# Reordering one recurrence step of a hybrid encoder kernel: a constant's load, the group norm's loads and buffers, and one piece of fill

## The chip, the cores and the metric

The kernel runs on one core of a Trainium2 chip. The metric is the device time of one execution in microseconds (us). The verdict between two kernels is the median of repeated runs. The profile is a hardware trace of one further execution.

The engines are TensorE (PE, matrix products), VectorE (DVE), ScalarE (ACT), GpSimd (POOL) and SyncE (SP). SP computes nothing here: it issues nearly all DMA transfers, one after the other, and when one of them has to wait, all behind it wait too.

## The reference, cut to what matters

One layer of an encoder is computed for 1024 + 256 = 1280 tokens of width 1024: a token mixer (a gated convolution and a bidirectional RWKV-7 recurrence, 8 heads of size 64), a gated feed-forward net and a gated embedding. The part around the change is the recurrence and the group norm of its result:

```python
def step(S, inp):
    r_t, w_t, kk_t, b_t, k_t, v_t = inp
    sa = jnp.einsum('bhvk,bhk->bhv', S, kk_t)
    S = (S * w_t[:, :, None, :] - sa[..., None] * b_t[:, :, None, :]
         + v_t[..., None] * k_t[:, :, None, :])
    return S, jnp.einsum('bhvk,bhk->bhv', S, r_t)
...
y = outs[0] + outs[1]
mean = jnp.mean(y, axis=-1, keepdims=True)
var = jnp.mean(jnp.square(y - mean), axis=-1, keepdims=True)
y = ((y - mean) * lax.rsqrt(var + GN_EPS)).reshape(bsz, T, D_RWKV) * gn_w + gn_b
bonus = jnp.sum(heads(r32) * heads(k32) * r_k, axis=-1, keepdims=True) * heads(v32)
g = jax.nn.sigmoid(gd.astype(f32)) @ gate_g2
out = (y + bonus.reshape(bsz, T, D_RWKV)) * g
```

## The kernel before, in words

The recurrence runs in chunks of 64 tokens. A step of the kernel handles two chunks (128 tokens) of one direction; there are 20 steps `n`: ten forward (0 to 9), then ten backward (10 to 19). They take the stretch from 337.5 us (the first product of step 0) to about 905 us of the trace.

Within a chunk the sequential sum is turned into products with the inverse of a triangular matrix. This inverse is made two steps ahead, in a chain that crosses four engines:

- `a_gram(n+2)`: PE makes Gram products (`g<-LS,K`), DVE masks them into `AT`, `LS` and `ZL`. SP stores `AT` to a scratch array `dA` (4 DMAs).
- `load_u(n+2)`: SP loads `dA` back as `U` in another layout (4 DMAs), and loads `W`, a constant that holds unit rows, from `in_consts`.
- `b_inv(n+2)`: POOL works in place on `W`, 31 pairs of a product (`tm<-W,U`) and a sum (`W<-W,tm`).
- `b_out(n+1)`, `b_back(n+1)`, in step `n`: SP stores `W` to `dW` (4 DMAs) and loads it as `MT` (4 DMAs).
- `b_d(n+1)`, later in step `n`: DVE transposes two blocks of `MT` into `Dm`.
- `b_x2(n+1)`: the first thing PE does in step `n+1`, `g<-Dm,AT`, reads `Dm`.

The step itself handles its two chunks with `c_p1`, `c_sa` and `c_z` (`ci` is 0, then 1). `c_p1` multiplies the state `SV` with `LS`, and ACT copies the result to `R`. `c_sa` multiplies `R` with `MT`, and ACT copies that into `SV` (`SV<-p`). `c_z` multiplies `SV` with `ZL`, and DVE makes the next state (`Sc<-p,Sc`, `SV<-Sc,pend`).

Between these pieces stands "fill": other projections of the layer (`mm<-U,wh`, `mm<-U,wl`), which depend on nothing in the recurrence. `gap(us, 1)` puts `us` worth of fill into PE's program, in pieces of about 0.8, and after each piece runs one more part of a Python generator `gn`. The total of the fill over a step is fixed by `share`; 18.6 is the sum of the arguments of a step's gaps.

From step 11 on, the generator is `group_norm`: each step normalizes the 128 tokens that the backward direction finished in the step before. It works on four 128x512 tiles: `y` and `y2` (the halves of the buffer tagged `cvp`), `v` and `q` (the halves of `cvy`). `gn_load` allocates both buffers and loads all four at the end of a step. The result goes into `y2` and from there to `d_ob`. Since the buffers are allocated anew, with one buffer for each tag, a load into them waits until the tile before is released.

The order of every engine is the order in which the Python code emits it (the wrapper `Pin` keeps program order). All instructions go through one helper, so the trace shows line L204 for all; they are told apart by their tiles.

Of the kernel before, what the change touches and what calls it, by code (L numbers as in the profile page):

```python
# [5 lines left out]
F32 = mybir.dt.float32  # L6
F32R = mybir.dt.float32r
AF = mybir.ActivationFunctionType
ALU = mybir.AluOpType
# [7 lines left out]
DC = 512  # L17
# [16 lines left out]
C_WI = C_BO + 128  # L34
C_N = C_WI + 256
# [24 lines left out]
class B:  # L60
# [5 lines left out]
    def sb(self, pool, shape, dt=F32, tag=None, bufs=None):  # L66
        kw = {} if bufs is None else dict(bufs=bufs)
        return pool.tile(shape, dt, name=tag, tag=tag, **kw)
# [57 lines left out]
def build(tc, I, O, dbg=None, upto=99):  # L126
    b = B(tc, I, O)
    nc = tc.nc
    sb = b.sb
    V, A, G, PE, SP = nc.vector, nc.scalar, nc.gpsimd, nc.tensor, nc.sync  # L130
# [45 lines left out]
    d_v, d_g = dram([2, T, 256], "d_v"), dram([2, T, 256], "d_g")  # L176
    d_y = [dram([2, T, 256], f"d_y{d}") for d in range(2)]
    d_ob = dram([T, DC], "d_ob")
# [13 lines left out]
    bon = sb(cp, [128, NT, 8], F32, "bon")  # L192
# [867 lines left out]
    st = {}  # L1060
# [39 lines left out]
    def a_gram(n, h):  # L1100
        d, g = steps[n]
        S = st[n]
        if h == 0:
            if n < 3:
                ZL[n] = sb(wk, [128, 2, 8, 128], F32, f"ZL{n}")
            S["AT"] = sb(wk, [128, 8, 64], F32, "AT", 3)
            S["dA"] = dr.tile([32, 32, 32], F32, name="dA", tag="dA", bufs=2)
        K, L, Zl, AT = S["K"], LS[n % 4], ZL[n % 3], S["AT"]
        bc = lambda c: cst[:, c:c + 64].unsqueeze(1).broadcast_to((128, 4, 64))
        MS, MQ = bc(C_MS[d]), bc(C_MQ[d])  # L1110
        pss = [sb(pg, [128, 4, 128], F32, "g") for par in range(2)]
        us = slice(4 * h, 4 * h + 4)
        for u in range(4):
            for par in range(2):
                rw = halves[par]
                PE.matmul(pss[par][:, u, :], K[rw, 4 * h + u, :], L[rw, par::2 - par, 4 * h + u, :], start=True, stop=True)
        cc, qc = slice(0, 64), slice(64, 128)
        for par in range(2):
            rw, ow, co, qo, ps = halves[par], halves[1 - par], par * 64, (1 - par) * 64, pss[par]
            V.tensor_tensor(AT[rw, us], ps[rw, :, cc], MS[rw], ALU.mult)  # L1120
            V.tensor_tensor(L[ow, par, us], ps[ow, :, cc], MS[ow], ALU.mult)
            V.tensor_tensor(Zl[:, par, us, qo:qo + 64], ps[:, :, qc], MQ, ALU.mult)
            if h == 1:
                for hh in range(2):
                    q = par * 2 + hh
                    SP.dma_start(S["dA"][q * 8:q * 8 + 8].rearrange("u s t -> s u t"), AT[q * 32:q * 32 + 32, :, hh * 32:hh * 32 + 32])
# [10 lines left out]
    def load_u(n):  # L1137
        Ut = st[n]["U"] = sb(wk, [128, 32, 32], F32, "U", 2)
        for r in range(4):
            SP.dma_start(Ut[r * 32:(r + 1) * 32], st[n]["dA"])  # L1140
        st[n]["W"] = sb(wk, [128, 8, 32], F32, "W", 2)
        SP.dma_start(st[n]["W"], I["consts"][:, C_WI:C_N].rearrange("p (c j) -> p c j", c=8))


    def b_inv(n):
# [137 lines left out]
            SP.dma_start(t[:, par * 256:(par + 1) * 256].rearrange("p (h v) -> p h v", v=64),  # L1283
                         I[nm][0].rearrange("(h p v) -> p h v", p=2, v=64)[par].unsqueeze(0).broadcast_to((128, 4, 64)))

    def gn_load(g):
        tk = slice(g * 128, (g + 1) * 128)
        ya, yb = sb(wq, [128, 2, DC], F32, "cvp"), sb(wq, [128, 2, DC], F32, "cvy")
        t4 = ya[:, 0], ya[:, 1], yb[:, 0], yb[:, 1]
        for t, src in zip(t4, (d_y[0], d_y[1], d_v, d_g)):  # L1290
            SP.dma_start(t.rearrange("t (q m) -> t q m", q=2), src[:, tk, :].rearrange("q t m -> t q m"))
        return t4

    def group_norm(g, t4):
        tk = slice(g * 128, (g + 1) * 128)
        y, y2, v, q = t4
        h8 = lambda t: t.rearrange("p (h v) -> p h v", v=64)
        bc = lambda t: t.unsqueeze(2).broadcast_to((128, 8, 64))
        V.tensor_tensor(y, y, y2, ALU.add)
        yield  # L1300
        mean = sb(wg, [128, 8], F32, "gm", 2)
        V.tensor_reduce(mean, h8(y), mybir.AxisListType.X, ALU.add)
        V.tensor_scalar(mean, mean, 1.0 / 64, None, ALU.mult)
        yield
        V.tensor_tensor(h8(y), h8(y), bc(mean), ALU.subtract)
        yield
        A.activation(y2, y, AF.Square)
        yield
        yield
        var = sb(wg, [128, 8], F32, "gv", 2)  # L1310
        V.tensor_reduce(var, h8(y2), mybir.AxisListType.X, ALU.add)
        V.tensor_scalar(var, var, 1.0 / 64, 64e-5, ALU.mult, ALU.add)
        V.tensor_tensor(h8(v), h8(v), bc(bon[:, g, :]), ALU.mult)
        yield
        s = sb(wg, [128, 8], F32, "grs")
        A.activation(s, var, AF.Sqrt)
        yield
        rs = b.newton(wg, var, s, 8, "gr", V)
        yield
        V.tensor_tensor(h8(y), h8(y), bc(rs), ALU.mult)  # L1320
        yield
        V.tensor_tensor(y, y, gnw, ALU.mult)
        yield
        V.tensor_tensor(y, y, gnb, ALU.add)
        yield
        V.tensor_tensor(y, y, v, ALU.add)
        yield
        pq = lambda t: t.rearrange("t (p h v) -> t p h v", p=2, v=64)
        V.tensor_tensor(y2.rearrange("t (h p v) -> t p h v", p=2, v=64), pq(y), pq(q), ALU.mult)
        SP.dma_start(d_ob[tk, :], y2)  # L1330

    go(9.0)
    for h in range(2):
# [25 lines left out]
    def gap(us, g=0):  # L1359
        k = max(1, round(us / 0.8))  # L1360
        for _ in range(k):
            fill.run(us * share / k)
            if g:
                next(gn, None)

    for n in range(N):
        share = max(0.0, fill.left - TAIL) / (N - n) / 18.6
        nx, nx2 = n + 1 < N, n + 2 < N
        run_side()
        load_l(n + 3)  # L1370
        b_x2(n)
        c_p1(n, 0)
        gap(1.3)
        if n >= 11:
            gn = group_norm(gl_g, gl_t)
        b_m21(n)
        c_keep(n, 0)
        if nx2:
            a_gram(n + 2, 0)
        gap(0.6)  # L1380
        c_sa(n, 0)
        if nx2:
            a_gram(n + 2, 1)
        gap(1.0)
        c_z(n, 0)
        if nx2:
            load_u(n + 2)
            b_inv(n + 2)
        gap(1.6, 1)
        c_p1(n, 1)  # L1390
        c_keep(n, 1)
        if nx2:
            a_t(n + 2)
        load_k(n + 3)
        if nx:
            b_out(n + 1)
        gap(1.0, 1)
        c_sa(n, 1)
        if nx:
            b_back(n + 1)  # L1400
        gap(1.5, 1)
        c_z(n, 1)
        fill.until(v_block + 1)
        if nx2:
            load_v(n + 2)
        gap(4.9, 1)
        if nx:
            b_d(n + 1)
        gap(6.7, 1)
        for _ in gn:  # L1410
            pass
        if n >= 10:
            gl_g = steps[n][1]
            gl_t = gn_load(gl_g)
    close(wk, pa, pg)


# [640 lines left out]
```

## Time and profile before

| | us |
|---|---|
| runs, without profile | 2200.03, 2207.47, 2580.53 |
| median of these | 2207.47 |
| the profiled execution | 2213.88 |
| its span, from the first to the last instruction | 2212.1 |

| engine | busy us | share of the span |
|---|---|---|
| PE | 2140.0 | 97% |
| DVE | 1343.1 | 61% |
| ACT | 888.4 | 40% |
| POOL | 520.5 | 24% |

The mean granted clock of TensorE is 0.989 of its full 2.4 GHz. Its lower level is 1.2 GHz, shown as 0.50. A row of the timeline gives the start and the length in us, the engine, the operation, out<-in by names, the shape and how many such instructions were merged; in brackets stands how long the engine was idle just before, and who ended that. A row of SPq is the issue of a DMA: its landing comes later. Where SP's row begins late, SP has waited.

### The profile page before, as it was taken

The page shows a single profiled execution, that of the slowest core. Times are in us where ns is not written, and L with a number is a line of the kernel's source. Part 1 is how long each engine was busy: PE and PEld are TensorE (multiplying, and loading weights), DVE is VectorE, ACT ScalarE, POOL GpSimd, SP SyncE. Part 2 cuts the span into 40 slices and gives each one's busy share as a digit, 9 for nine tenths or more (in the row PEclk, how much of TensorE's full clock was granted, in tenths as well). Part 3 has the DMA queues.
Part 4 walks back from the last instruction along what each step waited for, and adds up shares of the span by engine and source line. Part 5 has one row for each costly group of instructions (what it writes and reads, how often), then busy time and mean ns, then how long its engine had stood idle before and what let it go on. Part 6 is the DMA issues. An engine that isn't in the chain of part 4 may idle for free.

```text
span 2212.1 us, 40064 instructions
## 1 busy us (share of the span) xinstructions
PE 2140.0 (97%) x15929; PEld 1844.1 (83%) x15929; DVE 1343.1 (61%) x2198; ACT 888.4 (40%) x1529; POOL 520.5 (24%) x1378
## 2 busy tenths in 40 slices
PE   6999999999999999999999999999999999999998
PEld 5877798877777777888788999999999888887886
DVE  5467723444435555465577677776777765556565
ACT  5556513333334444422445444444444521113444
POOL 3000055777766667000000000000000011115000
PEclk9999999999999999999999999999999999999999
DMA  4346674554466665643436521222122432233121
GB/s 152 109 122 173 179 201 115 129 136 120 122 154 181 164 177 136 201 164 127 147 116 202 153 74 63 77 67 75 63 81 85 153 124 86 86 118 127 43 78 58
DMA packets 345877, 273.16 MB, mean 123 GB/s; under 512 B 135549, under 2 KB 306907, under 8 KB 345691
## 3 DMA queue, kind: packets, MB, share of 16 engines
q1 hardware_dynamic: 332859, 245.96, 38.0%
q10 hardware_dynamic: 9632, 13.11, 1.7%
q0 software_dynamic: 3200, 11.54, 1.5%
q8 instruction: 125, 2.05, 0.4%
q14 instruction: 61, 0.50, 0.1%
HBM read 187.18 MB, written 83.36 MB: 122 GB/s over the span
## 4 chain that ended last, share of the span: by engine, by line
PE 56%; DVE 6%; DMA 4%; ACT 2%; POOL 2%; issue 2%; SPq 1%; ACTq 0%; DVEq 0%; POOLq 0%
PE mm L204 23%; PE X L204 12%; PE Y L204 9%; PE g L204 6%; PE m L204 3%; PE p L204 2%; DVE h L204 1%; POOL W L204 1%; SPq L204 1%; POOL tm L204 1%; DVE wl L204 1%; DMA dW<-W 1%; DMA dA<-AT 1%; PE tp L204 1%; DMA MT<-dW 0%
## 5 line engine op out<-in xcount | busy, mean ns | idle before, releaser
L204 PE MATMUL mm<-U,wh 128*128 128x512 f32 (+1 forms) x1872 | 530.9, 371 | 2.9 <-ACT U L204 2.3
L204 PEld LDWEIGHTS mm<-U,wh 128*128 128x128 f32 x1872 | 324.1, 191 | 71.5 <-issue 12.0
L204 PE MATMUL mm<-U,wl 128*128 128x512 f32 (+1 forms) x936 | 338.1, 361 | 1.1 <-POOL wl L204 1.1
L204 POOL TENSOR_TENSOR tm<-W,U 128x60 f32<-128x60 f32 (+24 forms) x620 | 202.7, 327 | 141.2 <-DMA W<-in_consts 69.5
L204 POOL TENSOR_TENSOR W<-W,tm 128x60 f32<-128x60 f32 (+24 forms) x620 | 209.5, 338 | 48.6
L204 PEld LDWEIGHTS mm<-U,wl 128*128 128x128 f32 x936 | 178.8, 191 | 30.0 <-POOL wl L204 1.6
L204 DVE TENSOR_TENSOR f<-f,mm 128x512 f32<-128x512 f32 x200 | 136.4, 687 | 101.0 <-PE mm L204 99.9
L204 POOL TENSOR_TENSOR MG<-raw,MG 128x1024 fp32r<-128x1024 f32 x5 | 12.1, 2415 | 660.6 <-ACT MG L204 660.6
L204 DVE SCALAR_TENSOR_TENSOR h<-MGb,fcol,h 128x255 f32<-128x255 f32 (+1 forms) x176 | 152.4, 879 | 13.8 <-ACT h L204 12.0
L204 PE MATMUL X<-B,wh 128*128 128x384 f32 (+1 forms) x936 | 157.4, 314 | 2.7 <-DVE MGb L204 2.7
L204 PE MATMUL mm<-MG,act 128*128 128x512 f32 x600 | 158.3, 390 | 0.7 <-DVE f L204 0.6
L204 ACT CAST wh<-raw 128x512 fp32r<-128x512 f32 (+1 forms) x141 | 113.9, 809 | 108.9 <-PE Y L204 41.6
L204 PEld LDWEIGHTS X<-B,wh 128*128 128x128 f32 x936 | 143.4, 188 | 3.2 <-DVE MGb L204 3.2
L204 PE MATMUL X<-B,wl 128*128 128x384 f32 (+1 forms) x804 | 136.1, 313 | 2.9 <-DVE MGb L204 2.9
L204 PEld LDWEIGHTS mm<-MG,act 128*128 128x128 f32 x600 | 112.3, 188 | 24.9 <-DVE f L204 1.4
L204 PE MATMUL mm<-wh,MG 128*128 128x512 f32 x400 | 126.3, 394 | 0.0
L204 PEld LDWEIGHTS X<-B,wl 128*128 128x128 f32 x804 | 122.7, 188 | 3.2 <-DVE MGb L204 3.1
L204 PE MATMUL g<-WG,MG 128*128 128x512 f32 x480 | 112.8, 391 | 0.0
L204 DVE TENSOR_TENSOR AT<-g,cst 64x256 f32<-64x256 f32 x80 | 33.7, 421 | 121.5 <-PE g L204 119.5
L204 PEld LDWEIGHTS g<-WG,MG 128*128 128x128 f32 x480 | 89.4, 188 | 18.2
L204 DVE TENSOR_TENSOR wl<-raw,wh 128x1024 fp32r<-128x1024 f32 (+1 forms) x68 | 75.2, 1106 | 37.2 <-ACT wh L204 33.8
L204 PEld LDWEIGHTS mm<-wh,MG 128*128 128x128 f32 x400 | 74.9, 187 | 18.3
(502 smaller groups left out, 4181.0 us busy)
## 6 DMA issues: line engine op xcount, KB each, us to landing
raw<-in_w_up SPq DMA_DIRECT2D x53, 512.0 KB
raw<-in_w_in SPq DMA_DIRECT2D x39, 512.0 KB
d_act<-h SPq DMA_DIRECT2D x22, 640.0 KB
MGb<-d_act SPq DMA_DIRECT2D x20, 640.0 KB
raw<-in_w_down SPq DMA_DIRECT2D x22, 512.0 KB
d_bk<-o SPq DMA_DIRECT2D x32, 320.0 KB
U<-dA SPq DMA_DIRECT2D x80, 128.0 KB
K<-d_bk SPq DMA_DIRECT2D x19, 512.0 KB
```

The source lines that it names most:

```text
L204: return lambda *a, **k: tc.keep_in_program_order(f(*a, **k))
```

## The change

Four edits, all in the recurrence:

1. `W` for step `n+2` is allocated and loaded in `a_gram(n+2, 0)`, ahead of the stores of `AT`, and no longer in `load_u(n+2)` behind the loads of `U`.
2. The group norm's two buffers are allocated once and stay; a load then waits only for the half that it writes. The result is written over `v` and stored from there, not from `y2`.
3. At the end of a step only `y`, `y2` and `q` are loaded. `v` is loaded in the middle of the next step, behind the loads of `U` and ahead of `K`, `dW` and `MT`. The product of `v` with the bonus stands three parts later in the generator, which has one part more.
4. The gap behind `c_z(n, 0)` grows from 1.6 to 2.4, and the last gap of the step shrinks from 6.7 to 5.9.

```diff
@@ a_gram
             S["AT"] = sb(wk, [128, 8, 64], F32, "AT", 3)
             S["dA"] = dr.tile([32, 32, 32], F32, name="dA", tag="dA", bufs=2)
+            S["W"] = sb(wk, [128, 8, 32], F32, "W", 2)
+            SP.dma_start(S["W"], I["consts"][:, C_WI:C_N].rearrange("p (c j) -> p c j", c=8))
@@ load_u
-        st[n]["W"] = sb(wk, [128, 8, 32], F32, "W", 2)
-        SP.dma_start(st[n]["W"], I["consts"][:, C_WI:C_N].rearrange("p (c j) -> p c j", c=8))
@@ gn_load
-    def gn_load(g):
+    gts = []
+
+    def gn_load(g, which):
+        if not gts:
+            for tg in ("cvp", "cvy"):
+                t = sb(wq, [128, 2, DC], F32, tg)
+                gts.extend((t[:, 0], t[:, 1]))
         tk = slice(g * 128, (g + 1) * 128)
-        ya, yb = sb(wq, [128, 2, DC], F32, "cvp"), sb(wq, [128, 2, DC], F32, "cvy")
-        t4 = ya[:, 0], ya[:, 1], yb[:, 0], yb[:, 1]
-        for t, src in zip(t4, (d_y[0], d_y[1], d_v, d_g)):
-            SP.dma_start(t.rearrange("t (q m) -> t q m", q=2), src[:, tk, :].rearrange("q t m -> t q m"))
-        return t4
+        for i in which:
+            SP.dma_start(gts[i].rearrange("t (q m) -> t q m", q=2), (d_y[0], d_y[1], d_v, d_g)[i][:, tk, :].rearrange("q t m -> t q m"))
+        return gts
@@ group_norm
-        V.tensor_tensor(h8(v), h8(v), bc(bon[:, g, :]), ALU.mult)
         yield
         s = sb(wg, [128, 8], F32, "grs")
...
         V.tensor_tensor(y, y, gnb, ALU.add)
         yield
+        V.tensor_tensor(h8(v), h8(v), bc(bon[:, g, :]), ALU.mult)
+        yield
         V.tensor_tensor(y, y, v, ALU.add)
         yield
         pq = lambda t: t.rearrange("t (p h v) -> t p h v", p=2, v=64)
-        V.tensor_tensor(y2.rearrange("t (h p v) -> t p h v", p=2, v=64), pq(y), pq(q), ALU.mult)
-        SP.dma_start(d_ob[tk, :], y2)
+        V.tensor_tensor(v.rearrange("t (h p v) -> t p h v", p=2, v=64), pq(y), pq(q), ALU.mult)
+        SP.dma_start(d_ob[tk, :], v)
@@ the loop over steps
             b_inv(n + 2)
-        gap(1.6, 1)
+        if n >= 11:
+            gn_load(gl_g, (2,))
+        gap(2.4, 1)
         c_p1(n, 1)
...
-        gap(6.7, 1)
+        gap(5.9, 1)
         for _ in gn:
             pass
         if n >= 10:
             gl_g = steps[n][1]
-            gl_t = gn_load(gl_g)
+            gl_t = gn_load(gl_g, (0, 1, 3))
+    gn_load(gl_g, (2,))
```

SP's order in a step with a group norm, first of before, from the store of one group norm's result to the store of the next inverse:

```order
L204 DMA d_ob<-cvp 128x512
L204 DMA raw<-in_w_in 128x8x128
L204 DMA cvp<-d_y_65 128x2x256
L204 DMA cvp<-d_y_66 128x2x256
L204 DMA cvy<-d_v 128x2x256
L204 DMA cvy<-d_g 128x2x256
L204 DMA LS_2158<-d_c_60 64x4x128 x2
L204 DMA LS_2158<-d_q_62 128x4x128
L204 DMA dA<-AT 32x8x32 x4
L204 DMA U<-dA 32x1024 x4
L204 DMA W<-in_consts 128x256
L204 DMA K<-d_bk_58 128x4x256
```

And the same place of the changed kernel:

```order
L204 DMA d_ob<-cvy 128x512
L204 DMA cvp<-d_y_65 128x2x256
L204 DMA cvp<-d_y_66 128x2x256
L204 DMA cvy<-d_g 128x2x256
L204 DMA LS_2158<-d_c_60 64x4x128 x2
L204 DMA LS_2158<-d_q_62 128x4x128
L204 DMA W<-in_consts 128x256
L204 DMA dA<-AT 32x8x32 x4
L204 DMA U<-dA 32x1024 x4
L204 DMA cvy<-d_v 128x2x256
L204 DMA K<-d_bk_58 128x4x256
L204 DMA dW<-W 256x1x32 x4
```

The load of `W` has moved in front of the stores to `dA`, and the load of `v` has taken its place behind `U`. The store to `d_ob` reads another half than the loads behind it write.

PE's order in step 0, as a piece of the difference, around `c_p1(0, 1)`, which is the row of `SV,LS`:

```order
 L204 MATMUL mm<-U,wl 128x512
-L204 MATMUL p_3370<-SV,LS_2158 64x64 x8
+L204 MATMUL mm<-U,wh 128x512 x2
+L204 MATMUL mm<-U,wl 128x512
+L204 MATMUL p_3373<-SV,LS_2158 64x64 x8
 L204 MATMUL g<-cst,K 128x64 x16
```

One more triple of fill stands in front of that product.

ACT's order in a step with a group norm, from `R` of the second chunk on, first of before:

```order
L204 COPY R<-p_9103 128x256
L204 COPY Sc<-SV 64x256 x2
L204 COPY ZL_2273<-g 128x8x64 x2
L204 COPY SV<-p_9151 64x256 x2
L204 ACTIVATE gth<-mm 128x256
L204 DMA d_thr<-gth 128x256
L204 ACTIVATE cvp<-cvp 128x512
L204 COPY Y<-y 128x256
```

And of the changed kernel:

```order
L204 COPY R<-p_9106 128x256
L204 COPY Sc<-SV 64x256 x2
L204 COPY ZL_2273<-g 128x8x64 x2
L204 ACTIVATE gth<-mm 128x256
L204 DMA d_thr<-gth 128x256
L204 ACTIVATE cvp<-cvp 128x512
L204 COPY SV<-p_9155 64x256 x2
L204 COPY Y<-y 128x256
```

The group norm's square (`cvp<-cvp`) now stands ahead of the copies into `SV`, because three parts of the generator, not two, run before `c_p1(n, 1)`.

## Rows read from the trace of the kernel before

**Rows 1.** Windows, steps 0-9 and 11-18: stretch, length; busy by engine (instructions); PEclk, DMA share, GB/s.
```profile
337.50:617.60 280.10, 275.03 (x3565) 221.96 (x3565) 125.92 (x250) 89.85 (x205) 200.44 (x620) 0.99 0.50 123
645.10:884.90 239.80, 224.99 (x2801) 180.15 (x2800) 135.66 (x291) 106.89 (x212) 160.61 (x467) 0.95 0.62 166
```

**Rows 2.** Waits of PE, 290 to 905 us: who, for whom, us in total, times, longest.
```profile
PE g L204 <- DVE Dm L204: 13.2, 11, 3.1
PE p L204 <- DVE SV L204: 5.7, 6, 1.5
PE p L204 <- ACT SV L204: 1.0, 3, 0.4
```

**Rows 3.** Timeline of PE: two first products of a step, and one `c_p1(n, 1)`.
```profile
477.22 0.69 PE L204 MATMUL g<-Dm,AT 32*32 32x32 f32 x32
...
516.86 1.04 PE L204 MATMUL p<-SV,LS 128*64 128x64 f32 x16 [1.47 <-DVE SV L204]
...
768.40 0.31 PE L204 MATMUL g<-Dm,AT 32*32 32x32 f32 x2 [3.09 <-DVE Dm L204]
```

**Rows 4.** Timeline of SP in step 14, which begins at 737.7 us.
```profile
741.96 0.52 SPq L204 DMA_DIRECT2D d_ob<-cvp  x1
746.73 0.88 SPq L204 DMA_DIRECT2D cvp<-d_y  x2
...
748.17 0.47 SPq L204 DMA_DIRECT2D cvy<-d_g  x1
...
750.67 3.09 SPq L204 DMA_DIRECT2D dA<-AT  x4
757.17 1.74 SPq L204 DMA_DIRECT2D U<-dA  x4
758.95 0.42 SPq L204 DMA_DIRECT2D W<-in_consts  x1
...
759.90 2.56 SPq L204 DMA_DIRECT2D dW<-W  x4
```

**Rows 5.** Waits of SP, 290 to 905 us.
```profile
SPq L204 <- DMA d_ob<-cvp: 19.2, 8, 4.2
```

**Rows 6.** Timeline of DVE: step 5, then step 14.
```profile
471.54 0.43 DVE L204 STREAM_TRANSPOSE Dm<-MT 32x256 f32<-32x256 f32 x1 [2.13 <-DMA MT<-dW]
...
746.11 0.43 DVE L204 TENSOR_TENSOR AT<-g,cst 64x256 f32<-64x256 f32 x1
...
750.29 0.77 DVE L204 TENSOR_TENSOR cvp<-cvp 128x512 f32<-128x512 f32 x1 [1.74 <-DMA cvp<-d_y]
...
767.91 0.43 DVE L204 STREAM_TRANSPOSE Dm<-MT 32x256 f32<-32x256 f32 x1 [5.97 <-DMA MT<-dW]
```

**Rows 7.** Timeline of POOL: the end of one inverse and the start of the next.
```profile
754.46 0.22 POOL L204 TENSOR_TENSOR W<-W,tm 128x8 f32<-128x8 f32 x1
762.42 0.24 POOL L204 TENSOR_TENSOR tm<-W,U 128x31 f32<-128x31 f32 x1 [7.75 <-DMA W<-in_consts]
```

**Rows 8.** Waits of POOL, 280 to 960 us.
```profile
POOL tm L204 <- DMA W<-in_consts: 69.5, 11, 22.0
```

**Rows 9.** Windows: one of six stretches at half clock, and the sum of the six.
```profile
705.77:716.01 10.24, 9.65 (x110) 7.41 (x113) 4.74 (x8) 2.64 (x7) 8.57 (x22) 0.50 0.86 247
...
sum 30.73, PE 28.20 PEld 21.71 DVE 9.62 ACT 8.90 POOL 19.93; mean PE 4.70 PEld 3.62 DVE 1.60 ACT 1.48 POOL 3.32
```

**Rows 10.** Timeline of PE: two matmuls of fill at half clock, and two at full.
```profile
709.84 1.05 PE L204 MATMUL mm<-U,wh 128*128 128x512 f32 x2
...
728.52 0.62 PE L204 MATMUL mm<-U,wh 128*128 128x512 f32 x2
```

**Rows 11.** Timeline of ACT and PE in step 14: the copies into `SV`, the square, the product behind.
```profile
752.63 0.75 ACT L204 COPY SV<-p 64x256 f32<-64x256 f32 x2
753.41 0.63 ACT L204 ACTIVATE cvp<-cvp 128x512 f32<-128x512 f32 x1
...
753.44 0.69 PE L204 MATMUL p<-SV,ZL 128*64 128x64 f32 x16 [0.40 <-ACT SV L204]
```

## The prediction

> **What bounds the kernel now.** The page of the profile comes first: PE is busy for 97% of the span, so the time is PE's work plus what holds PE up. All four edits lie in the recurrence, and they add and remove no work of PE. I therefore read PE in that stretch alone, by windows over steps 0 to 9 and steps 11 to 18 [rows 1]. Ten early steps take 280.1 us (28.0 each) at a mean clock of 0.99. Eight late steps take 239.8 us (30.0 each) at 0.95, and PE is idle there for 14.8 us, against 5.1 us before. The late steps are the ones with a group norm. The reader should see that at most two us a step are in question.
>
> The second view is the list of what PE waited for [rows 2]. The largest entry, 13.2 us, is the first product of a step, which waits for `Dm`; the next, 5.7 us in six pieces, is the product of `c_p1(n, 1)`, which waits for the state that DVE makes. All of PE's waits in the recurrence are 19.9 us.
>
> The third view is the granted clock. Six stretches, 30.7 us together, ran at 1.2 GHz instead of 2.4 [rows 9], and the one shown begins at 705.77, just behind a wait for `Dm`. Two fill matmuls took 1.05 us there and 0.62 us at the full level [rows 10]. PE was busy for 28.2 us of the six stretches; work at half the clock takes twice as long, so about 14.1 us were lost. A page of the Trainium skill, "TensorE: Matmul & The Clock Gate", section "Seeing it yourself", warns that the clock events in a trace have been seen to be unreliable; by that, this loss could be 0. The durations of rows 10 speak for a real one.
>
> The fourth view tells why `Dm` is late: SP's order of time in step 14 [rows 4], beside DVE [rows 6] and POOL [rows 7]. DVE finished the last `AT` at 746.54 (746.11 + 0.43). SP came to store it only at 750.67, because it had stood between 742.48 and 746.73, waiting for `d_ob` to land before `cvp` could be loaded again, and then issued four loads of the group norm and three of `LS`. That wait alone is 19.2 us over eight steps [rows 5]. `U` followed at 757.17, and `dW`, whose inverse POOL had finished at 754.68 [rows 7], at 759.90: 5.2 us late, standing in SP's queue. `Dm` came 8.0 us behind that, at 767.91, and PE idled for 3.09 us, from 765.31 to 768.40 [rows 3]. In step 5, without a group norm, `Dm` was begun at 471.54 and wanted at 477.22: 5.7 us to spare.
>
> **The change, part by part.**
>
> *Group norm's buffers, and `v` later.* In step 14 the loads of `y`, `y2` and `q` no longer wait for `d_ob`, so they begin at 742.5. Three issues of 0.47 and the `LS` issues (about 2.0 us between the end of the last group norm load, 748.64, and `dA`, 750.67) end at 745.9; with `W` (0.42) SP is free at 746.4, just about when `AT` is ready. So `dA` goes out near 746.6, 4.1 us sooner; `U` and what is behind it follow. Behind `U` the load of `v` (0.47) stands where `W` (0.42) stood. `dW` would be issued near 755.8, `Dm` begun near 763.8 instead of 767.9, and wanted at 765.3: the wait is gone, with 1.5 us to spare. I keep 1.5 us of residue over all late steps and book 13.2 - 1.5 = **11.7 us** [rows 2]. Bounds: 0 (SP stands elsewhere instead) and 13.2.
>
> *Unit rows earlier.* The waits of POOL name `W` with 69.5 us [rows 8], and that invites too large a gain. `W` was issued directly behind `U`, so without it POOL waits for `U`, issued only 0.42 us sooner. PE does not wait for POOL but for `Dm`; in the early steps 5.7 us of spare time cover it. I book 0 beyond what the part above contains; bounds 0 and 0.42 in each of the eight late steps, 3.4.
>
> *Fill moved.* On average 0.8 us more fill stands ahead of `c_p1(n, 1)`. The six waits for the state average 0.95 us, the longest is 1.47 [rows 2, 3]; 0.8 off each, where there is as much, leaves about 1.4 us. Gain **4.3 us**; bounds 0 and 5.7. At the end of the step 0.8 us of cover goes, between `b_d` and the next `g<-Dm`. In the early steps it comes out of 5.7 us of spare time. In the late steps the first product keeps its place in the step, since the sum of the gaps is the same; only `b_d` stands 0.8 us later in DVE's order, and DVE waited 5.97 us there for `MT` [rows 6]. Cost 0, as long as `MT` is what comes last.
>
> *Clock.* Of the 14.1 us lost at half clock I take four fifths as coming back with the waits that stood before the falls: **11 us**. Bounds 0 and 14.1.
>
> *What is added.* The square of the group norm (0.63 us on ACT) now stands in front of the copies into `SV` in nine steps, 11 to 19. PE waits for just these copies behind `c_sa(n, 1)`, and in step 14 it already idled 0.40 us for them [rows 11]. The price lies between 0 (ACT has room) and 0.63 x 9 = 5.7 us. I take 0.4 x 9 = 3.6, since ACT and PE ran level in the row, and one further fall of the clock, half of 3.4 us (a ninth of the 30.7 us of rows 9): together **5 us** of loss.
>
> *Without a price.* The bonus product is moved, not added. DVE's reduction behind the square now stands ahead of the second `Sc`, but `Sc` needs the `SV` copies (0.75) and a product (0.69) after the square as well. `v` doubles the bytes between `U` and `dW` (256 KB for 128 KB); a load of 256 KB took 3.6 us from its issue at 746.73 to its first use at 750.29 [rows 4, 6], so half of that, 1.8 us a step, bounds what it can add to `dW`. I take 0, because `U` and `K` (512 KB each) are in front of `dW` either way; the bound feeds the first rival.
>
> Sum: -11.7 - 4.3 - 11 + 5 = **-22 us**. The profiled execution took 2213.88 us, so it would take 2192. It lies 6.4 us above the median of the runs, 2207.47, which is therefore forecast at 2185.5; I say **2186**.
>
> **The rivals.**
>
> 1. *Half of it.* SP is free in time, but the transfers are not: `dA` lands behind 768 KB of group norm loads, and `v` adds up to 1.8 us ahead of `dW`. The 1.5 us of spare time worked out above are then used up, and half of the waits for `Dm` and of the clock's loss stays: -5.9 - 4.3 - 5.5 + 5 = -11, **2197**. For it: the load at 746.73 took 3.6 us to be usable. Against: the loads leave 4.2 us sooner, too.
> 2. *Nothing.* The waits move to another place of the step, and what one edit gives another takes: within 4 us of 2207. For it: PE's work is unchanged, 94% busy even in the late steps [rows 1]. Against: the two waits have different causes, each of them removed.
> 3. *Slower: the square blocks ACT.* ACT works in order. Between the landing of `y` and `y2` and the square stand about 3.1 us of DVE work (750.29 to 753.41 [rows 6, 11]). If they still land as late as in step 14, where DVE idled 1.74 us for them, the copies into `SV` end at 753.41 + 0.63 + 0.75 = 754.8 and not at 753.4: 1.4 us more of PE's idle time in each of nine steps, 12.6 us, and with a fall of the clock each time (1.7 us) 15 more. With 4 us from the moved fill that gives -4 + 28, **2231**. It decides once `y` and `y2` land later than 3.1 us before ACT has copied `ZL`. Against it: these loads leave 4.2 us earlier, and the larger gap gives DVE 0.8 us more.
> 4. *The clock term is empty.* The half clock of the records is not what cost time, as the page named above allows: -11.7 - 4.3 + 3.6, about -12, **2195**. Rows 10 speak against it.
> 5. *More than forecast.* All waits [rows 2] and all of the clock's loss vanish at no cost: 19.9 + 14.1 = 34 us, **2173**.
>
> That the change does not do what it says is no rival: the orders ahead show the moved rows.
>
> **Chances.** Forecast (2178 to 2194) 0.55; half 0.18; nothing 0.10; slower by the square 0.09; empty clock term 0.04; more than forecast 0.04. The range that holds 8 in 10 reaches from the full gain, 2172, to just above no change, 2209; it leaves out the slower rival and a few per cent at either end. About 2% (44 us) is what a measurement of this kernel can tell from no change: below 2163 or above 2252. All waits together are worth 34 us, so faster by 2% has 0.02; the slower rival at twice its price per step has 0.02; the rest, 0.96, is within 2%.
>
> **What the profile of the changed kernel would show.** If the chain is right, SP has no wait for `d_ob` in the recurrence, `dA` is issued within 1 us of the last `AT` in the late steps, and PE's waits for `Dm` are under 3 us. If the moved fill is right, the waits of `p<-SV,LS` for the state are under 2 us. If the clock term is right, at most two stretches at 0.50 are left between 330 and 905 us. The added cost would show as waits of `p<-SV,ZL` for ACT of 3 to 6 us, up from 1.0; above 10 us the third rival holds. POOL should then name `U` where it named `W`. The forecast fails if `dA` stays late though SP is free, or if the late steps still take 30 us.

## The result, and the profile after

The changed kernel takes 2188.16 us, the median of 7 runs (2184.22 to 2198.98). The kernel before, on the same chip, took 2209.37 (7 runs). The ratio is 0.9924, with a 95% interval from 0.9905 to 0.9943: a small gain that is measured, and far from 2%. The ratio is formed from the fast runs alone (one run before, of 2580.53 us, was slow) and is not the quotient of the two medians, which is 0.9904. The forecast was 2186 in a range from 2172 to 2209. The two profiled executions took 2213.88 and 2190.42 us, 23.5 apart. From the first product of step 0 to that of step 19 they differ by 19.2 us; the rest lies outside the recurrence, in code that is the same in all fourteen kernels profiled here and took between 1655 and 1665 us in them.

First the windows, with the columns of [rows 1]: steps 0 to 9, steps 11 to 18, and the one stretch at half clock that is left in the recurrence.

```profile
335.60:608.40 272.80, 270.79 (x3565) 219.60 (x3564) 125.82 (x250) 89.74 (x205) 199.65 (x620) 1.00 0.50 125
635.60:863.80 228.20, 216.90 (x2800) 173.97 (x2799) 136.57 (x291) 105.87 (x212) 165.71 (x467) 0.99 0.64 173
...
782.38:785.79 3.41, 3.41 (x22) 2.46 (x20) 0.60 (x1) 1.02 (x3) 2.78 (x9) 0.50 0.74 222
```

Against [rows 1] the early steps lost 7.3 us and the late ones 11.6. The second number is PE's busy time, and it is the one to look at. With the same number of instructions (but for one record) it fell from 275.03 to 270.79 and from 224.99 to 216.90, 12.3 us together. Nothing was taken from PE, but two things are in this number. One is the clock: the half-clock time went from 30.7 us in six stretches [rows 9] to 3.4 us in one. The other is a wait that the list of PE's waits does not hold. The early steps had a single half-clock stretch of 3.4 us, and yet the products `p<-SV,LS` were busy there for 2.2 us less, though one of them took as long as before (groups of instructions, before and after):

```profile
L204 PE MATMUL p<-SV,LS 128*64 128x64 f32 x320 | 16.8, 229 | 4.4 <-DVE SV L204 4.0
L204 PE MATMUL p<-SV,LS 128*64 128x64 f32 x320 | 14.6, 228 | 1.8 <-DVE SV L204 1.6
```

DVE and PE in step 1, before and after:

```profile
375.08 0.87 DVE L204 TENSOR_TENSOR SV<-Sc,pend 64x256 f32<-64x256 f32 x2
375.64 1.04 PE L204 MATMUL p<-SV,LS 128*64 128x64 f32 x16
...
372.82 0.88 DVE L204 TENSOR_TENSOR SV<-Sc,pend 64x256 f32<-64x256 f32 x2
374.08 0.69 PE L204 MATMUL p<-SV,LS 128*64 128x64 f32 x16
```

DVE writes the state in two halves. Before, PE began its 16 products with the first half and stood after the first few until the second was there, at 375.95. The products that were already running cover most of this stand, so it counts as busy time, and the row takes 1.04 us in place of 0.69. All ten early `c_p1(n, 1)` were lengthened like this, and seven of the eight in steps 11 to 18; after the change three and two are. That is 4.0 us of the 12.3; the other 8.3 are left for the clock.

The rest of what the two windows lost, 6.6 us, is idle time of PE. The list of what PE waited for, 290 to 905 us, says whose:

```profile
PE g L204 <- DVE Dm L204: 5.0, 8, 0.9
PE p L204 <- ACT SV L204: 4.5, 7, 1.0
PE p L204 <- DVE SV L204: 2.0, 5, 0.8
PE p L204 <- ACT R L204: 1.0, 1, 1.0
PE y L204 <- ACT SV L204: 0.5, 1, 0.5
```

Beside [rows 2], `Dm` fell from 13.2 to 5.0 us and the state from 5.7 to 2.0; the waits for ACT rose from 1.0 to 6.0, of which 1.0 is a wait for `R`. All together 19.9 became 13.0.

SP's timeline in step 14 (which now begins at 721.3 us) is the answer to [rows 4]:

```profile
726.23 0.52 SPq L204 DMA_DIRECT2D d_ob<-cvy  x1
726.80 1.04 SPq L204 DMA_DIRECT2D cvp<-d_y  x2
727.89 0.52 SPq L204 DMA_DIRECT2D cvy<-d_g  x1
728.46 1.24 SPq L204 DMA_DIRECT2D LS<-d_c  x2
729.74 1.55 SPq L204 DMA_DIRECT2D LS<-d_q  x1
731.33 0.50 SPq L204 DMA_DIRECT2D W<-in_consts  x1
732.54 3.67 SPq L204 DMA_DIRECT2D dA<-AT  x4
738.31 1.99 SPq L204 DMA_DIRECT2D U<-dA  x4
740.34 0.42 SPq L204 DMA_DIRECT2D cvy<-d_v  x1
740.81 0.47 SPq L204 DMA_DIRECT2D K<-d_bk  x1
741.32 2.75 SPq L204 DMA_DIRECT2D dW<-W  x4
747.94 2.05 SPq L204 DMA_DIRECT2D MT<-dW  x4
```

DVE, POOL and PE around it, as in [rows 6], [rows 7] and [rows 3]:

```profile
729.70 0.43 DVE L204 TENSOR_TENSOR AT<-g,cst 64x256 f32<-64x256 f32 x1
...
734.72 0.69 DVE L204 TENSOR_TENSOR cvp<-cvp 128x512 f32<-128x512 f32 x1 [2.42 <-DMA cvp<-d_y]
...
739.52 0.22 POOL L204 TENSOR_TENSOR W<-W,tm 128x8 f32<-128x8 f32 x1
...
750.25 0.43 DVE L204 STREAM_TRANSPOSE Dm<-MT 32x256 f32<-32x256 f32 x1 [2.34 <-DMA MT<-dW]
...
751.91 0.69 PE L204 MATMUL g<-Dm,AT 32*32 32x32 f32 x30 [0.94 <-DVE Dm L204]
```

The stand of 4.2 us between the store of a result and the next load of `y` is gone. But the last `AT` ends at 730.13 and `dA` goes out 2.4 us behind it, not within 1 us: the chunk's rows of `LS` and `W` are still ahead. Between the first issue of `dA` and the first of `U` lie 5.8 us (6.5 before). So of the 4.1 us that the prediction gave to `dA`, 1.7 came in this step. Step 14 was the latest of all before the change. Over steps 11 to 17 the first `dA` had gone out 0.43 us behind the end of the last `AT` in the mean (from 1.33 us ahead of it, since the first two of the four stores need only the first half of `AT`, to 4.13 behind); now it goes out 0.31 us ahead of it. `dW` now goes out about 1.6 us behind POOL's last sum, where it was 5.2.

SP's wait for `d_ob`, 290 to 905 us:

```profile
SPq L204 <- DMA d_ob<-cvy: 10.1, 5, 3.8
```

So SP still waits for it, against the sign that the prediction named ([rows 5]: 19.2). But 9.2 of the 10.1 us fall behind 840 us, three times at the load of `v`, with nothing urgent right behind it. And POOL's waits, 280 to 960 us:

```profile
POOL tm L204 <- DMA U<-dA: 62.7, 13, 21.2
```

POOL names `U` where it named `W` [rows 8], as expected.

### The profile page after: what moved, and what is told of

The parts are those of the page before. It is cut to its first block, busy times and chain, and to the rows that moved or that the text cites. A ratio compares the mean times of both kernels' runs of the same rounds, so it can differ in the third digit from the quotient of the medians.

```text
span 2188.6 us, 40030 instructions
## 1 busy us (share of the span) xinstructions
PE 2124.6 (97%) x15929; PEld 1832.3 (84%) x15929; DVE 1343.8 (61%) x2198; ACT 886.4 (41%) x1529; POOL 524.9 (24%) x1378
## 4 chain that ended last, share of the span: by engine, by line
PE 62%; DVE 6%; DMA 4%; ACT 3%; issue 2%; POOL 2%; SPq 1%; ACTq 0%; DVEq 0%; POOLq 0%
PE mm L204 27%; PE X L204 12%; PE Y L204 9%; PE g L204 7%; PE m L204 3%; PE p L204 3%; DVE h L204 1%; POOL tm L204 1%; POOL W L204 1%; PE y L204 1%; DVE wl L204 1%; SPq L204 1%; PE tp L204 1%; DMA dW<-W 1%; DVE aj L204 0%
## 5 line engine op out<-in xcount | busy, mean ns | idle before, releaser
L204 PEld LDWEIGHTS g<-WG,MG 128*128 128x128 f32 x480 | 89.4, 188 | 18.2
```

The lines of the kernel that those rows point to most:

```text
L204: return lambda *a, **k: tc.keep_in_program_order(f(*a, **k))
```

## The experiments

All ratios are to the kernel before, run on the same chip, with 95% intervals. In the diffs a minus is the changed kernel, unless said otherwise.

**One edit undone at a time.** The first leaves `W` where it was:

```diff
@@ a_gram
-            S["W"] = sb(wk, [128, 8, 32], F32, "W", 2)
-            SP.dma_start(S["W"], I["consts"][:, C_WI:C_N] ...)
@@ load_u, behind the loads of U
+        st[n]["W"] = sb(wk, [128, 8, 32], F32, "W", 2)
+        SP.dma_start(st[n]["W"], I["consts"][:, C_WI:C_N] ...)
```

> The change with one edit undone: the unit rows W are loaded behind U again. Theory (the late steps were slow because SP stood behind the store of the group norm's result; POOL's wait for W only names the last of two loads 0.42 us apart): within 4 us of the changed kernel's 2188, PE's waits for Dm stay at 4 to 7 us, and POOL names W again instead of U. Rival (W held POOL, and its earlier load gave the gain): 2196 or more, with PE's waits for Dm back above 10 us.

2195.6 us, 0.9951 [0.9933, 0.9968], between the two forecasts. So by this run the load of `W`, to which the prediction gave nothing of its own, holds 0.27 of the 0.76%. The windows view of steps 11 to 18:

```profile
639.30:877.30 238.00, 224.03 (x2800) 179.38 (x2799) 137.49 (x292) 105.76 (x212) 163.69 (x469) 0.96 0.62 167
```

And POOL's waits, where `W` is named as before:

```profile
POOL tm L204 <- DMA W<-in_consts: 74.4, 14, 22.3
```

The late steps took 238.0 us; the early ones stayed at 272.8. This profiled execution, 2203.1 us, was the longest of its seven, so 238.0 is more than is typical. The waits for `Dm` were 8.4 us and the half-clock time 20.5.

The second undoes the group norm's part (buffers, result over `v`, `v` in mid step, order of the generator):

```diff
@@ gn_load
-        for i in which:
-            SP.dma_start(gts[i].rearrange(...), ...)
+        ya, yb = sb(wq, [128, 2, DC], F32, "cvp"), sb(wq, [128, 2, DC], F32, "cvy")
+        t4 = ya[:, 0], ya[:, 1], yb[:, 0], yb[:, 1]
+        for t, src in zip(t4, (d_y[0], d_y[1], d_v, d_g)):
+            SP.dma_start(t.rearrange(...), ...)
@@ group_norm
-        V.tensor_tensor(v.rearrange(...), pq(y), pq(q), ALU.mult)
-        SP.dma_start(d_ob[tk, :], v)
+        V.tensor_tensor(y2.rearrange(...), pq(y), pq(q), ALU.mult)
+        SP.dma_start(d_ob[tk, :], y2)
```

> The change with the group norm's edits undone (buffers allocated anew, result over y2, all four loads at the end of the step, the bonus product at its old place); W early and the fill moved stay. Theory: SP's wait for d_ob is back at 15 to 25 us, PE's waits for Dm back at 11 to 16 us, three or more stretches at half clock between 290 and 890 us; 2200 to 2207. Rival (the moved fill or W gave the gain): within 4 us of 2188.

2195.55 us, 0.9946 [0.9931, 0.9962]: between the forecast 2200 to 2207 and its rival. SP waits for the store as it did:

```profile
SPq L204 <- DMA d_ob<-cvp: 20.2, 8, 5.0
```

`Dm` cost PE 7.1 us in place of 5.0, and not the 11 to 16 expected. The late steps took 229.7, hardly more than the 228.2 of the change, so most of the lost 7 us is not in this profile of them.

The third undoes the moved fill:

```diff
-        gap(2.4, 1)
+        gap(1.6, 1)
         c_p1(n, 1)
...
-        gap(5.9, 1)
+        gap(6.7, 1)
```

> The change with the gaps at 1.6 and 6.7 again; with them the square of the group norm goes back behind the copies into SV. Theory: PE's waits for the state (p<-SV,LS on DVE) are back at 4 to 7 us, up from 2.0, the waits for ACT's copies fall from 5.0 to below 2, so the two cancel but for the clock: 2187 to 2194. Rival (the moved fill is the larger part of the gain): 2198 or more.

2196.34 us, 0.9954 [0.9938, 0.9969], again between the forecasts. Early and late steps:

```profile
336.90:617.00 280.10, 274.98 (x3567) 222.12 (x3566) 126.02 (x250) 89.64 (x205) 199.61 (x622) 0.99 0.49 122
644.50:870.60 226.10, 215.81 (x2800) 173.59 (x2799) 135.88 (x289) 106.69 (x212) 166.59 (x466) 1.00 0.65 175
```

The early stretch is at its old length to the tenth, and the waits for the state are back at 5.8 us; the waits inside the products, too, are those of before, in ten and seven steps. The copies of ACT cost 1.0 us again: what the prediction put on the square comes with the moved fill.

**One edit alone**, each put into the kernel before.

> The kernel before with the moved fill alone (gaps 2.4 and 5.9; the group norm's square then stands in front of the copies into SV). Undoing one of the three edits cost 7 to 8 us each, so the edits look additive. Additive: 2197 to 2201, steps 0 to 9 take 273 us, steps 11 to 18 keep 238 to 243 us with waits for Dm of 11 us or more and several stretches at half clock. Rival (each is worth something only beside the others): 2204 to 2209.

> The kernel before with W loaded early alone. Additive: 2199 to 2203, from the late steps, waits for Dm 8 to 11 us; the time from U's issue to POOL's first product falls from 5.7 to about 4.5 us in steps 11 to 18. Rival (POOL's wait is only renamed, and 0.42 us a step is hidden by the early steps' spare time): 2204 to 2209.

> The kernel before with the group norm's edits alone (buffers stay, result over v, v loaded in mid step). Additive: 2198 to 2202, SP's wait for d_ob below 8 us, waits for Dm 8 to 11 us. The prediction's own attribution (all of the Dm gain lies here): 2190 to 2196, waits for Dm below 6 us. Rival (nothing alone): 2204 to 2209.

| put in alone | us | ratio | steps 0-9 | steps 11-18 | PE waits `Dm` | half clock |
|---|---|---|---|---|---|---|
| fill | 2197.03 | 0.9956 [0.9935, 0.9976] | 272.9 | 234.6 | 9.6 | 10.2 |
| `W` | 2202.67 | 0.9986 [0.9970, 1.0002] | 280.2 | 229.4 | 9.4 | 10.2 |
| group norm | 2199.45 | 0.9964 [0.9949, 0.9980] | 278.7 | 231.5 | 7.7 | 13.7 |
| (before) | | 1 | 280.1 | 239.8 | 13.2 | 30.7 |
| (all) | 2188.16 | 0.9924 [0.9905, 0.9943] | 272.8 | 228.2 | 5.0 | 3.4 |

All three times came out as the additive forecasts had them. With the fill alone the late steps (238 to 243 expected) and the waits for `Dm` (11 or more) were below the forecast, with the group norm's edits alone the waits for `Dm` (8 to 11), just. The last four columns are of one profiled execution each: 2195.33, 2199.32, 2202.32, 2213.88 and 2190.42 us, from the top. That with `W` is the shortest of its runs and that of before 4.5 us above its median, so the late steps make `W` look better than the times do.

Alone the three are worth 0.44, 0.14 and 0.36%, 0.94 together; undone, they cost 0.30, 0.27 and 0.22%, 0.79 together; the whole is 0.76. Each of these has an uncertainty of about 0.2, so nothing shows that the edits do not add up. `W` alone does not clear its interval. But these runs, with the kernel before and the changed one, are all eight combinations of the three edits, so each edit stands in four pairs of kernels that differ in nothing else. The gain in each pair, in per cent:

| edit | alone | beside one of the others | beside both | mean |
|---|---|---|---|---|
| fill | 0.44 | 0.40 (`W`), 0.13 (group norm) | 0.30 | 0.32, or 7 us |
| `W` | 0.14 | 0.10 (fill), 0.10 (group norm) | 0.27 | 0.15, or 3.4 us |
| group norm | 0.36 | 0.05 (fill), 0.32 (`W`) | 0.22 | 0.24, or 5 us |

All twelve are gains. By the intervals of the single ratios a mean has an uncertainty of about 0.15, an estimate, so the value of `W` is at the edge of what can be told. The moved fill alone explains the early steps entirely.

**The square back behind the copies**: in the generator it comes one part later, so that ACT does the `SV` copies first.

```diff
-        A.activation(y2, y, AF.Square)
         yield
+        A.activation(y2, y, AF.Square)
         yield
```

> The changed kernel with one yield moved, so that the square of the group norm stands behind the copies into SV on ACT again while the fill stays moved. Theory (the square in front costs what the prediction booked as 5 us): PE's waits for ACT's SV fall from 5.0 us to below 2, and the time by 3 to 6 us, to 2182 to 2185. Rival (PE would wait for Dm at the next step instead): PE's waits for Dm grow by as much, and the time stays at 2187 to 2190.

2186.81 us, 0.9912 [0.9892, 0.9932]: the intervals overlap, and the 2182 to 2185 that were expected were missed. The waits for ACT fell as they should:

```profile
PE p L204 <- ACT SV L204: 1.6, 6, 0.4
```

That is 2.9 us less of waits for the copies, and no more for `Dm` (4.8), and the median went down by 1.4: the cost of the square is real in the trace, and too small to be told in the time.

**Where `v` is loaded, and where the result goes.** First `v` behind `q` at the end of a step, with the rest of the change kept:

```diff
-        if n >= 11:
-            gn_load(gl_g, (2,))
...
-            gl_t = gn_load(gl_g, (0, 1, 3))
+            gl_t = gn_load(gl_g, (0, 1, 3, 2))
```

> The change with one part undone: v is loaded at the end of the step again, behind y, y2 and q; the buffers stay, and the result still goes over v, so that this load waits for d_ob to land. Theory (SP's wait for d_ob is what the group norm's edits took away): the wait is back at 15 to 25 us, and the time goes to 2192 to 2197, as with all of them undone (2195.6). Rival (the wait for d_ob is covered by the wait for AT, and what counts is that the loads of y and y2 leave early): 2186 to 2190.

2187.23 us, 0.9903 [0.9879, 0.9926], as the rival had it. SP waits for the store again,

```profile
SPq L204 <- DMA d_ob<-cvy: 14.2, 6, 3.4
```

and it costs nothing that can be measured, though `LS`, `W` and `dA` stand behind it: in step 14 the first `dA` goes out 4.8 us behind the last `AT`, later than before the change. Then `v` as in the change, but the result in `y2`:

```diff
-        V.tensor_tensor(v.rearrange(...), pq(y), pq(q), ALU.mult)
-        SP.dma_start(d_ob[tk, :], v)
+        V.tensor_tensor(y2.rearrange(...), pq(y), pq(q), ALU.mult)
+        SP.dma_start(d_ob[tk, :], y2)
```

> The change with one part undone: the group norm's result goes into y2 again and is stored from there, so that the load of y2, second of three at the end of a step, waits for d_ob to land; the buffers stay and v is loaded in mid step. The run with v last had SP's wait for d_ob back at 14 us and yet took 2187. Theory (the wait hurts only where y2, the first operand that DVE needs, stands behind it): the wait for d_ob is 14 to 22 us and the time 2192 to 2197. Rival (the wait for d_ob costs nothing anywhere, and what the group norm's edits gave lies in loading fewer bytes ahead of dA or in the moved bonus product): 2185 to 2190.

2193.32 us, 0.9945 [0.9925, 0.9965], as expected, with this wait of SP:

```profile
SPq L204 <- DMA d_ob<-cvp: 22.1, 7, 4.1
```

Here `y2`, the second load in the row, stands behind the wait, and with it `q`, `LS`, `W` and `dA`. The waits for `Dm` stayed at 4.9 us. What PE felt in step 14 came by the square, which waits for `y2`, and by the copies into `SV` behind it (DVE's first operation of the group norm, then the square on ACT, then PE):

```profile
735.81 0.69 DVE L204 TENSOR_TENSOR cvp<-cvp 128x512 f32<-128x512 f32 x1 [3.61 <-DMA cvp<-d_y]
...
738.25 0.63 ACT L204 ACTIVATE cvp<-cvp 128x512 f32<-128x512 f32 x1 [1.84 <-DVE cvp L204]
...
739.58 1.03 PE L204 MATMUL p<-SV,ZL 128*64 128x64 f32 x16 [2.37 <-ACT SV L204]
```

A stretch at half clock begins at 739.73, right behind this wait. It is what the prediction's third rival described, in one step. The late steps went from 228.2 to 231.3, with 10.2 us of half clock. The medians differ by 5 us and the intervals overlap; since the ratio is that of the run without any of the group norm's edits (0.9946), it leans to "the result over `v` is what helps, not the later load of `v`".

**What stands between `U` and `dW`.** The square back, and `q` beside `v` in mid step:

```diff
-            gn_load(gl_g, (2,))
+            gn_load(gl_g, (2, 3))
...
-            gl_t = gn_load(gl_g, (0, 1, 3))
+            gl_t = gn_load(gl_g, (0, 1))
```

> The change with the square behind the copies into SV, and q loaded in mid step beside v, so that 256 KB less stand ahead of dA in the late steps. Theory (dA lands late because the group norm's loads are ahead of it; from its last issue to U's first issue it takes 3.2 us in the late steps, 1.9 in the early ones): this falls to 2.5 or less, PE's waits for Dm from 5.0 to below 4, and the time is 2181 to 2185. Rival (it is not the bytes): 3 us again, and 2185 to 2189, as with the square alone.

2196.1 us, 0.9949 [0.9929, 0.9969], against both forecasts: the median is 9 us above the square back alone, for one load of 256 KB that went from ahead of `dA` to ahead of `dW`. `Dm` cost 8.7 us and the half-clock time was 17.1, in an execution of 2190.42 us, one of the shortest of its twelve.

The next goes further: the loads of `LS`, too, move from the start of the step to behind `U`, so that nothing of them stands ahead of `dA`.

```diff
-        load_l(n + 3)
...
             load_u(n + 2)
             b_inv(n + 2)
+        load_l(n + 3)
```

> As the run with q in mid step, and the three loads of LS for three steps ahead stand behind U, too, so that in every step 512 KB and three issues (1.9 us of SP) less stand ahead of dA. Theory (SP's queue and the bytes ahead of dA set when the inverse starts): from the last AT to U's first issue 3 us or less in the late steps instead of 5.3, waits for Dm below 3 us, 2178 to 2184. Rival (LS is then late for the Gram products, or K and dW behind it wait longer): 2187 or more, with a wait of PE for LS, or dW issued later behind POOL's end than the 1.05 us of now.

2209.7 us, 1.0014 [0.9997, 1.0031]: the whole gain is lost, as the rival had it. SP's timeline in step 14:

```profile
747.86 1.71 SPq L204 DMA_DIRECT2D U<-dA  x4
749.61 1.72 SPq L204 DMA_DIRECT2D LS<-d_c  x2
751.37 0.60 SPq L204 DMA_DIRECT2D LS<-d_q  x1
752.02 0.51 SPq L204 DMA_DIRECT2D cvy<-d_v  x1
752.57 0.47 SPq L204 DMA_DIRECT2D cvy<-d_g  x1
753.14 0.41 SPq L204 DMA_DIRECT2D K<-d_bk  x1
753.65 5.90 SPq L204 DMA_DIRECT2D dW<-W  x4
...
761.26 0.83 SPq L204 DMA_DIRECT2D MT<-dW  x2
```

The end of the inverse on POOL, then DVE and PE behind it:

```profile
749.70 0.22 POOL L204 TENSOR_TENSOR W<-W,tm 128x8 f32<-128x8 f32 x1
...
763.71 0.43 DVE L204 STREAM_TRANSPOSE Dm<-MT 32x256 f32<-32x256 f32 x1 [4.98 <-DMA MT<-dW]
764.20 0.31 PE L204 MATMUL g<-Dm,AT 32*32 32x32 f32 x2 [2.79 <-DVE Dm L204]
```

The inverse is done at 749.92, `dW` goes out at 753.65, and its four issues take 5.90 us instead of 2.75. PE waited 18.2 us for `Dm` in all, with 34.1 us of half clock: worse in both than before the change.

**`K` behind `MT` as well**: the square back, `v` at the end, and `K` issued only after `MT`, so that `dW` follows `U` directly.

```diff
-        load_k(n + 3)
...
         b_back(n + 1)
+        load_k(n + 3)
```

> The change with v loaded at the end of the step and the square behind the copies into SV (each alone left the time at 2187), and K, 512 KB, loaded behind MT instead of ahead of dW, so that nothing stands between U and dW on SP. The run with LS, v and q there lost all of the gain (2209.7, dW issued 6.9 us behind POOL's end), the one with q and v there 9 us. Theory (the late steps hang on the path from POOL's end through dW and MT to Dm, and what is queued ahead of dW lengthens it): from dW's first issue to MT's first issue 4.5 to 5 us in the late steps instead of 5.5 to 6, PE's waits for Dm below 3 us, 2178 to 2184. Rival (POOL's inverse, 26.7 us of a step of 28, ends too late anyway): waits for Dm at 4 to 5 us and 2184 to 2188. Second rival (K then comes too late for the Gram products two steps on): a wait of PE for K, 2190 or more.

2187.33 us, 0.9905 [0.9886, 0.9924], against the 2178 to 2184 expected. SP's timeline in step 14:

```profile
738.04 1.83 SPq L204 DMA_DIRECT2D U<-dA  x4
740.10 2.56 SPq L204 DMA_DIRECT2D dW<-W  x4
744.13 1.82 SPq L204 DMA_DIRECT2D MT<-dW  x4
746.00 0.45 SPq L204 DMA_DIRECT2D K<-d_bk  x1
```

`MT` now follows `dW` after 4.0 us (6.6 in the change), and nothing comes of it: no time, and no less waiting for `Dm` (6.1 us). SP waited 21.1 us for `d_ob` here, more than before the change, without a loss of time. What was won behind the inverse had gone over to other links, as the next part shows.

## Why the prediction was right, and which terms were mis-sized

Booked against measured, in the pair of profiles (the 5 us that the prediction added are 3.6 of waits and 1.4 of clock, and stand here in two lines):

| term | booked | measured |
|---|---|---|
| waits for `Dm` | -11.7 | -8.2 |
| waits for the state, as listed | -4.3 | -3.7 |
| waits for the state inside the products | none | -4.0 |
| half clock | -9.6 | -8.3 |
| waits for ACT | +3.6 | +5.0 |
| sum | -22 | -19.2 |

The half clock is what is left of PE's busy time in the two windows, so that the sum meets the 19.2 us of the recurrence proves nothing by itself. That the whole fell by 23.5 owes 4 us to the stretches around it. The forecast time came out in part by luck: `Dm` and the clock were booked too large by 4.8 us together, a term of 4.0 was not seen, and 4 us came from outside. Point by point:

*The moved fill* was right, and larger than its entry: it took away the waits for the second half of the state, too. All kernels without it have the lengthened products in ten early and seven late steps, all kernels with it in three and two. Without the other two edits it brings 0.44%.

*The clock* was right in kind, and the fourth rival falls: with the waits inside the products taken off, PE's busy time for the same instructions still dropped by 8.3 us, and one stretch was left where at most two were named. The prediction's 14.1 us of loss was too much. "Twice as long" is not what its own rows 10 show: 1.05 us against 0.62 is 1.7 times, which makes 11.5 us of the 28.2. For the five of the six stretches that lie in the two windows (24.8 us of PE's work), and the one after, the same ratio gives a gain of 8.7 us, an estimate that agrees with the 8.3. The page of the Trainium skill "TensorE: Matmul & The Clock Gate", section "Seeing it yourself", says that clock events in traces have been seen to be unreliable. Here they agree with the durations: without a loss at half clock the recurrence would have gained the 10.9 us of waits, and it gained 19.2.

*The square* was priced about right: 3.6 us were booked, and the waits for the copies in front of `p<-SV,ZL` grew by 3.5. It comes with the moved fill, as expected: 4.6 us of such waits with the fill alone, 1.0 with the fill where it was (third run).

*The group norm's buffers* were the right cause of the wait for `d_ob`, but not of all of the lateness. Its sign, under 3 us of waits for `Dm`, was missed (5.0). The step that failed is "`dA` goes out near 746.6, 4.1 us sooner; `U` and what is behind it follow". In the late steps the mean time from the last `AT` to the first issue of `U` went only from 5.70 to 5.32 us. The 4.1 us were read from step 14 alone, the latest of the late steps; in the mean the first `dA` had stood 0.43 us behind the last `AT`, and it came 0.7 us sooner. In the four pairs that differ in the group norm's edits alone, `U` came 0.9 to 2.3 us sooner, 1.4 in the mean; the load of `W` in front of `dA` puts back 0.6 in the mean of its pairs.

*`W`* is a mis-sized term: 0, at most 3.4 us, were booked; the four pairs give 3.4 us in the mean, from 2 to 6. The argument was that POOL does not hold up PE and that `W` costs 0.42 us of issue. The first half is true in the early steps only. To see why, follow one inverse around: from a step's start to the last `AT`, to `U`, through POOL, to `dW`, to `Dm`, to the start of the step two later. The means in us, each link from the rows' starts and ends in the timelines, of the inverses for steps 13 to 19 but for the first line (steps 3 to 10):

| | start to `AT` | `AT` to `U` | `U` to POOL | inverse | to `dW` | `dW` to `Dm` | spare | half the sum |
|---|---|---|---|---|---|---|---|---|
| after, early | 9.09 | 2.39 | 5.17 | 25.73 | 0.52 | 8.34 | 3.31 | 27.28 |
| before | 11.23 | 5.70 | 5.95 | 26.23 | 1.74 | 9.81 | -0.21 | 30.22 |
| after | 10.14 | 5.32 | 4.51 | 26.85 | 1.05 | 10.04 | -0.22 | 28.85 |
| `W` undone | 11.40 | 4.05 | 5.03 | 26.48 | 3.33 | 10.28 | -0.27 | 30.14 |
| `q` in mid step | 11.14 | 4.15 | 4.58 | 26.50 | 2.36 | 10.47 | -0.24 | 29.48 |
| `LS` late | 11.86 | 2.86 | 4.72 | 26.10 | 6.85 | 10.30 | -0.15 | 31.26 |
| `v` at the end | 9.80 | 5.56 | 5.33 | 26.74 | 0.27 | 9.31 | -0.23 | 28.39 |
| `K` late | 10.12 | 6.67 | 5.41 | 26.94 | 0.03 | 7.98 | -0.29 | 28.43 |

Each line is one profiled execution. That of `W` undone is 7.5 us above its median and that of before 4.5, that of `q` in mid step 5.7 below; differences of a few tenths in one link are not told from chance.

Half the sum is the length of a step. In the early steps 3 to 4 us are left over and the fill sets the length: a sooner `W` or `dW` changes nothing there. In the late steps nothing is left over: the step is as long as half of this loop, nearly half of which is the inverse itself. So a microsecond on any link costs half a microsecond in each late step, if the other links stay as they are, and whatever of it PE sees as a wait may bring a fall of the clock on top. Where `W` gains is less clear than its wait on POOL suggests. In its four pairs the link from `U` to POOL changed by -1.03, -0.12, +0.10 and -0.52 us, -0.4 in the mean, which is the 0.42 us of its issue that the prediction named. The link from POOL's end to `dW` fell by 0.8 in the mean: `W` no longer stands between `U` and `dW` in SP's queue. Which link carries the gain was not isolated.

The table also tells the tried reorderings apart. `LS` behind `U` does bring `U` 2.5 us sooner, and `dW` then stands in SP's queue 5.8 us longer. `K` late takes 3 us from the links behind POOL, and the two ahead of POOL grow by 1.35 and 0.9. In the run with only `v` at the end they stood at 5.56 and 5.33; why `U` comes later was not tried. The reading of [rows 5] is corrected by three runs. With `v` at the end SP's wait for `d_ob` stands ahead of `dA`; the two links ahead of POOL are 1.1 us longer than in the change, and the two behind POOL's end 1.5 shorter, with no load of `v` ahead of `dW` any more. With `K` late the wait was 21.1 us, and nothing was lost. With the result in `y2` about as much waiting went with a time 5 us longer, and there `y2` itself came late.

*The rivals.* The first had its mechanism partly present (`dA` did not come as much sooner as SP was free), but the time that it gave, 2197, is out; so are the second, no gain, and the fifth, 2173. The third does not hold (6.0 us of waits for ACT, where it needed more than 10). What no run isolates: how much of each edit's gain is waiting and how much is clock. The run with `K` late has 9.7 us of listed waits and 10.2 at half clock, the change 13.0 and 3.4.

No version tried beats the change beyond its interval: the square back, `v` at the end and `K` late lie within 1.4 us of it.

## What to carry to other kernels

When a chain made ahead feeds a step, add up its links over its whole way round before saying that an engine in it "is not waited for": where nothing is spare, every link counts, in part, whichever wait the profile names. For an in-order issuing queue ask of each wait what stands behind it; 14 us of waiting cost nothing here in one place, where what was lost ahead of the inverse was won back behind it, and a single load between `U` and `dW` cost 9 us in another. Read more than one step before pricing a delay: the one shown may be the worst. And where PE is 95% busy, count its busy time for the same instructions: that is where well over half of the recurrence's gain lay. A shorter row of the same products can be a faster clock, or a wait inside the row that the list of waits leaves out.

## What the runs showed of the hardware

- Short waits were worth more than their own length. 10.9 us of waits left the recurrence, 6.9 listed and 4.0 inside products, and 19.2 us of time: the stretches at half clock went with them. In all fourteen profiles each such stretch between 290 and 905 us began inside a wait of PE or within 2.0 us of the end of one. They do not follow the waits strictly: in the change, where no wait was longer than 1.0 us, one began 0.8 us behind a wait of 0.85; in the run with the fill undone a wait of 2.08 us had none behind it.
- A wait inside a row of products did not show as idle time of PE: the 16 products `p<-SV,LS` took 1.04 us with it and 0.69 without, at 0.23 us for a single one.
- The four stores `dA` (32 KB each) were usable by the load behind them 3.2 us after the start of the last issue in the late steps of the change (3.1 before) and 1.9 in the early ones. The DMA share was 0.64 against 0.50 in the windows above; that this is the reason was not tried.
- Four issues of `dW` took 2.75 us of SP in step 14 of the change, and 5.90 in step 14 of the run with `LS` late, behind six loads issued in the 4.0 us before them.
